# Two products in place of three for four more weight matrices of an encoder layer, and the memory tokens prepared later

## The chip, the core and the metric

The kernel runs on one core of a Trainium2 chip. The metric is the device time of one execution in microseconds (us); lower is better. The kernel before takes 1872.16 us, the median of 3 runs (1871.98 to 1872.21).

## What is computed

One layer of a hybrid encoder on 256 tokens of 2048 features, all in float32, with 256 memory tokens:

```python
for i in range(DEPTH):                       # DEPTH is 1
    u = rmsnorm(h, mix_norm[i])
    h = h + ssd_mixer(u, ...)                # w_in, conv, Mamba-2 scan both ways, norm, w_out
    h = h + mem_cross_attention(rmsnorm(h, xattn_norm[i]), mem_n, wq, wkv, wo)   # 4 heads of 512
    h = h + conv_glu_ffn(rmsnorm(h, ffn_norm[i]), w_up, conv_w, conv_b, w_down)
return rmsnorm(h, final_norm)
```

`mem_n` is the rmsnorm of the memory tokens. `w_out` has 4096 x 2048 weights, `wq` and `wo` 2048 x 2048, `wkv` 2048 x 4096 (keys, then values), `w_up` 2048 x 11264, `w_down` 5632 x 2048.

## The kernel before

**Operands in two parts.** Every float32 operand is split into two float32r parts: a high part (a cast, ScalarE, `split_plain` L106 or `split_scaled` L101) and a low part (operand minus high part, VectorE, L107 or L102). A product of two operands is high x high + high x low + low x high. An activation operand lives in "units": `new_unit` (L94) gives a tile of 4 feature tiles by 2 parts by 256 tokens, high and low side by side; a pool holds 11 of them.

**Weights** stream from HBM in loads of 512 KB (`load_raw` L109, ring of 5 `raw` tiles), are split into `w_hi` and `w_lo` (128 x 1024 each, rings of 4), and go to TensorE as the stationary operand in blocks of 128 x 128. SyncE (SP) issues these loads in order.

**Two forms of the product with features on the partitions.** For each weight block, `gemm_feat` (L132) issues three products with 256 columns: `w_hi` with the operand's high part, `w_hi` with its low part, `w_lo` with the high part (L152 to L154). A `psg` tile of two PSUM banks takes 4 feature tiles, so 512 output features. `gemm_feat_wide` (L157) issues two: `w_hi` with both parts at once, 512 columns (L169), and `w_lo` with the high part, 256 columns (L171). Its output has two halves that must be added (L173 on ScalarE, L174 on VectorE), and a `psg` holds 256 output features. There are two `psg` tiles. Before the change only `w_up` uses the wide form; `w_in`, `w_out`, `wq`, the keys' half of `wkv` and `wo` use three products. Values and `w_down` go through `gemm_tok` (L176), which has the operand stationary and 512 weight columns moving.

**Order of the work.** The source is in program order; a scheduler of the framework then orders each engine's queue by simulated readiness and program priority, and every engine runs its queue in order. Sequence: x is transposed and split; per group of 512 inner features `project` / `project_z` (`w_in`) and `scan_group` (the scan, 8 groups) make one unit `units_y[g]`; `inv_rms` (L223) turns the sum of squares into `r_ssd`, 1/rms of the scan's output, on every partition; the memory tokens are loaded, normed, transposed and split (L491 to L518) in a pool of their own; `w_out` (L527 to L533), whose result is multiplied by `r_ssd`, added to the residual `hT` and split into `units_xa` by `residual_units` (L476); queries, keys, values and attention head by head; `wo`; the FFN. `hT` comes back from DRAM with one 2 MB load (L524).

Of the kernel before, what the change touches and what calls it, by code (L numbers as in the profile page):

```python
# [36 lines left out]
def kernel(  # L37
# [28 lines left out]
    def psum_g():  # L66
        """two banks"""
        return sb(ps_g, [P, 2, 512], "psg")
# [16 lines left out]
    # tri[:, 0, l] = 1 where l >= m, tri[:, 1, l] = 1 where l <= m  # L85
# [46 lines left out]
    def gemm_feat(units, wv, cols, k_first=0, first_raw=None):  # L132
        """features on the partitions: banks of two 128-feature tiles by 256 tokens"""
        width = sum(n for _, n in cols)
        nft = width // P
        kc = 1024 // width
        nk = 4 * len(units)
        ps = psum_g()
        banks = [ps[:, b, :] for b in range((nft + 1) // 2)]
        for k0 in range(0, nk, kc):  # L140
            hi, lo = load_weights(wv, k_first + k0, cols, first_raw if k0 == 0 else None)
            for kk in range(kc):
                kt = k0 + kk
# [12 lines left out]

    def gemm_feat_wide(units, wv, c0, dst):  # L157
        """dst [P, 2, T] = two 128-feature tiles; the high part of the weights meets both parts of the
        operand in one product, so each tile has a bank whose halves add up to it"""
        nk = 4 * len(units)  # L160
        ps = psum_g()
        for k0 in range(0, nk, 4):
            hi, lo = load_weights(wv, k0, [(c0, 2 * P)])
            for kk in range(4):
                kt = k0 + kk
                unit = units[kt // 4]
                for ft in range(2):
                    fs = slice(ft * P, (ft + 1) * P)
                    nc.tensor.matmul(ps[:, ft, :], hi[:, kk, fs], unit[2][:, kt % 4].rearrange("p s t -> p (s t)"),  # L169
                                     start=(kt == 0), stop=False, skip_group_check=True)  # L170
                    nc.tensor.matmul(ps[:, ft, :T], lo[:, kk, fs], unit[0][:, kt % 4, :], start=False,  # L171
                                     stop=(kt == nk - 1), skip_group_check=True)
        nc.scalar.copy(out=dst, in_=ps[:, :, T:])  # L173
        nc.vector.tensor_tensor(out=dst, in0=ps[:, :, :T], in1=dst, op=ALU.add)  # L174

    def gemm_tok(units, wv, c0, k_first=0):  # L176
        """tokens on the partitions: two banks of 128 tokens by 512 features"""
# [23 lines left out]
    def add_square(pool, acc, src2, first):  # L201
        """src2: [P, 2, T]"""
# [7 lines left out]
    def rsqrt_mean(pool, dst, total, n, tags=("rs_v", "rs_s")):  # L210
        """dst = (total / n + eps) ** -0.5: a square root from the table, then one Heron step"""
# [60 lines left out]
        # the column of 1/rms as a row on every partition  # L272
# [12 lines left out]
    with tc.tile_pool(name="ssd", bufs=1) as ssd:  # L285
        acc_y = sb(ssd, [P, 2, T], "acc_y")

# [10 lines left out]
        # log1p(ex) = ln(w) * ex / (w - 1) with w = 1 + ex, and ex itself where w == 1  # L298
# [32 lines left out]
        # decay to the end of the chunk times dt: forward for chunk 0, backward for chunk 1  # L331
# [12 lines left out]
        # exp(cum) where a state comes in: forward rows in chunk 1, backward rows in chunk 0  # L344
# [9 lines left out]
        def conv_silu(banks, f0s, dst):  # L354
            """centred conv of 4 taps over the tokens, bias, silu; two feature tiles per bank"""
# [33 lines left out]
        def scan_group(g, xs, bc, sz):  # L389
# [5 lines left out]
            # token-major x and B  # L395
# [15 lines left out]
            # state that leaves chunk 0 forwards, and the one that leaves chunk 1 backwards  # L411
# [5 lines left out]
            for c in range(2):  # L417
# [8 lines left out]
                # of the two exponents the one of the direction that reaches l from m is <= 0, the other >= 0  # L426
# [14 lines left out]
                # what the incoming state gives, before its decay  # L441
# [34 lines left out]
    def residual_units(pool, hT, banks, u, gname, acc_t, r=None):  # L476
        unit = new_unit()
        for b, bank in enumerate(banks):
            hv = hT[:, u * 4 + 2 * b:u * 4 + 2 * b + 2, :]
            if r is None:  # L480
                nc.vector.tensor_tensor(out=hv, in0=two(bank), in1=hv, op=ALU.add)
            else:
                t = sb(pool, [P, 2, T], "res_t", bufs=2)
                nc.vector.tensor_tensor(out=t, in0=two(bank), in1=rows2(r), op=ALU.mult)
# [5 lines left out]

# [1 line left out]
    units_mem = [new_unit() for _ in range(4)]  # L492
    with tc.tile_pool(name="memp", bufs=1) as memp:
        mt = []
        for tt in range(2):
            m = sb(memp, [P, D], f"mem{tt}")
            nc.sync.dma_start(out=m, in_=mem[tt * P:(tt + 1) * P, :])
            ss = sb(memp, [P, 4], f"mss{tt}")
            for q4 in range(4):
                junk = sb(memp, [P, 512], "junk")  # L500
                nc.scalar.activation(out=junk, in_=m[:, q4 * 512:(q4 + 1) * 512], func=AF.Square,
                                     accum_out=ss[:, q4:q4 + 1])
            rs = sb(memp, [P, 1], f"mrs{tt}")
            tot = sb(memp, [P, 1], f"mtot{tt}")
            nc.vector.tensor_reduce(out=tot, in_=ss, axis=AX.X, op=ALU.add)
            rsqrt_mean(memp, rs, tot, D)
            nc.vector.tensor_scalar(out=m, in0=m, scalar1=rs, scalar2=None, op0=ALU.mult)
            mt.append(m)
        for u in range(4):
            for jj in range(2):  # L510
                ps = psum_m()
                for j in range(2):
                    kt = u * 4 + jj * 2 + j
                    for tt in range(2):
                        nc.tensor.transpose(out=ps[:, j * T + tt * P:j * T + (tt + 1) * P],
                                            in_=mt[tt][:, kt * P:(kt + 1) * P], identity=ident)
                for j in range(2):
                    split_scaled(units_mem[u], jj * 2 + j, two(ps)[:, j, :], pcol("g_mem", u * 4 + jj * 2 + j))  # L518

    with tc.tile_pool(name="res", bufs=1) as res:  # L520
# [4 lines left out]
        with tc.tile_pool(name="att", bufs=1) as att:  # L525
# [4 lines left out]
            for u in range(4):  # L530
                banks = gemm_feat(units_y, w_out_v, [(u * 512, 512)])
                units_xa.append(residual_units(att, hT, banks, u, "g_xa", acc_h, r_ssd))
            inv_rms(att, acc_h, r_xa, D)  # L533

            wkv_v = kview(wkv)
# [4 lines left out]
            # 1/rms of the queries' tokens as columns: it goes into the scale of the softmax  # L540
# [14 lines left out]

            def query(hd):
                return split_banks(pair("q", [P, 4, T]), gemm_feat(units_xa, wq_v, [(hd * 512, 512)]))

            def key(hd):
                return split_banks(pair("k", [P, 4, T]), gemm_feat(units_mem, wkv_v, [(hd * 512, 512)]))  # L560
# [7 lines left out]
            def three(out_ap, lhsT, rhs, first, last):  # L568
                """one product of operands in two parts each; lhsT, rhs: (hi, lo)"""
# [56 lines left out]
            for u in range(4):  # L626
                banks = gemm_feat(units_o, wo_v, [(u * 512, 512)])
                units_ffn.append(residual_units(att, hT, banks, u, "g_ffn", acc_f))
            inv_rms(att, acc_f, r_ffn, D)

# [1 line left out]
        with tc.tile_pool(name="ffn", bufs=1) as ffn:  # L632
# [6 lines left out]
            def ffn_unit(i):  # L639
                sg = sb(ffn, [P, 4, T], "sg")  # L640
                for b in range(2):
                    s = sb(ffn, [P, 2, T], "f_s", bufs=2)
                    gemm_feat_wide(units_ffn, w_up_v, i * 512 + b * 256, s)
# [13 lines left out]
                for b in range(2):  # L657
                    bs = slice(2 * b, 2 * b + 2)
                    s = sb(ffn, [P, 2, T], "f_s", bufs=2)
                    gemm_feat_wide(units_ffn, w_up_v, FFN + i * 512 + b * 256, s)  # L660
# [25 lines left out]
            # the table of the square root, loaded before the last rows need it  # L686
# [70 lines left out]
```

## Time and profile before

| what | value |
|---|---|
| median of 3 runs | 1872.16 us |
| span of the profiled execution (first to last instruction) | 1870.4 us |
| around the span, against the median | 1.8 us |
| TensorE busy | 1851.4 us, 99% |
| VectorE busy | 1246.3 us, 67% |
| ScalarE busy | 1007.2 us, 54% |
| mean granted TensorE clock | 0.998 of 2.4 GHz |

The times in the trace are counted from the first instruction of the span. "Busy" of TensorE is the union of its products' records, which overlap, since a product's record runs on while the next one streams; what a product costs in a stream is therefore read from the distance of starts. The profiled execution has no time of its own beyond its span; the 1.8 us is the difference to the median.

### The profile page before, as it was taken

The page shows a single profiled execution, that of the slowest core. Times are in us where ns is not written, and L with a number is a line of the kernel's source. Part 1 is how long each engine was busy: PE and PEld are TensorE (multiplying, and loading weights), DVE is VectorE, ACT ScalarE, POOL GpSimd, SP SyncE. Part 2 cuts the span into 40 slices and gives each one's busy share as a digit, 9 for nine tenths or more (in the row PEclk, how much of TensorE's full clock was granted, in tenths as well). Part 3 has the DMA queues.
Part 4 walks back from the last instruction along what each step waited for, and adds up shares of the span by engine and source line. Part 5 has one row for each costly group of instructions (what it writes and reads, how often), then busy time and mean ns, then how long its engine had stood idle before and what let it go on. Part 6 is the DMA issues. An engine that isn't in the chain of part 4 may idle for free.

```text
span 1870.4 us, 31851 instructions
## 1 busy us (share of the span) xinstructions
PE 1851.4 (99%) x12845; PEld 1715.6 (92%) x12845; DVE 1246.3 (67%) x1764; ACT 1007.2 (54%) x1434; POOL 2.3 (0%) x11
## 2 busy tenths in 40 slices
PE   8999999999999999999999999999999999999997
PEld 8999999999999999999999998888888888888886
DVE  7778878988887756554454557666664556666654
ACT  6666767766675544444444446555553345555443
POOL 0000000000000000000000000000000000000000
PEclk9999999999999999999999999999999999999999
DMA  8667666766756655555555556566655565656553
GB/s 288 197 201 214 205 197 195 220 199 183 224 183 223 230 188 181 181 161 178 171 178 172 165 182 202 180 189 188 189 191 194 195 192 185 189 184 189 188 195 113
DMA packets 256947, 359.06 MB, mean 192 GB/s; under 512 B 11616, under 2 KB 145120, under 8 KB 256288
## 3 DMA queue, kind: packets, MB, share of 16 engines
q1 hardware_dynamic: 256720, 356.76, 60.8%
q8 instruction: 100, 1.64, 0.4%
q14 instruction: 47, 0.39, 0.1%
q0 software_dynamic: 80, 0.28, 0.0%
HBM read 352.60 MB, written 4.39 MB: 191 GB/s over the span
## 4 chain that ended last, share of the span: by engine, by line
PE 99%; DMA 0%; DVE 0%; ACT 0%; SPq 0%; issue 0%; DVEq 0%
PE psg L169 18%; PE psg L154 17%; PE psg L152 16%; PE psg L153 16%; PE psg L171 9%; PE psm L190 6%; PE psm L191 6%; PE psm L189 6%; PE psm L449 1%; PE psm L444 1%; PE psm L415 1%; PE psm L572 0%; PE psm L570 0%; PE psm L571 0%; DMA x<-in_x_dram 0%; PE psm L401 0%
## 5 line engine op out<-in xcount | busy, mean ns | idle before, releaser
L107 DVE TENSOR_TENSOR w_lo<-raw,w_hi 128x1024 fp32r<-128x1024 f32 x618 | 753.4, 1223 | 518.4 <-ACT w_hi L106 515.7
L106 ACT CAST w_hi<-raw 128x1024 fp32r<-128x1024 f32 x618 | 645.1, 1048 | 697.7 <-PE psg L153 255.0
L154 PE MATMUL psg<-unit,w_lo 128*128 128x256 f32 x2576 | 733.4, 285 | 0.0
L152 PE MATMUL psg<-unit,w_hi 128*128 128x256 f32 x2576 | 731.6, 284 | 0.0
L153 PE MATMUL psg<-unit,w_hi 128*128 128x256 f32 x2576 | 730.3, 284 | 0.0
L154 PEld LDWEIGHTS psg<-unit,w_lo 128*128 128x128 f32 x2576 | 494.3, 192 | 3.4 <-issue 3.1
L152 PEld LDWEIGHTS psg<-unit,w_hi 128*128 128x128 f32 x2576 | 494.4, 192 | 1.7 <-issue 1.7
L153 PEld LDWEIGHTS psg<-unit,w_hi 128*128 128x128 f32 x2576 | 494.5, 192 | 0.3 <-issue 0.2
L169 PE MATMUL psg<-unit,w_hi 128*128 128x512 f32 x1408 | 493.5, 396 | 0.0
L171 PE MATMUL psg<-unit,w_lo 128*128 128x256 f32 x1408 | 393.2, 279 | 0.0
L169 PEld LDWEIGHTS psg<-unit,w_hi 128*128 128x128 f32 x1408 | 264.3, 188 | 63.6
L171 PEld LDWEIGHTS psg<-unit,w_lo 128*128 128x128 f32 x1408 | 265.2, 188 | 0.1
L189 PE MATMUL psm<-w_hi,unit 128*128 128x512 f32 x480 | 186.8, 389 | 0.0
L190 PE MATMUL psm<-w_lo,unit 128*128 128x512 f32 x480 | 186.8, 389 | 0.0
L191 PE MATMUL psm<-w_hi,unit 128*128 128x512 f32 x480 | 186.8, 389 | 0.0
L189 PEld LDWEIGHTS psm<-w_hi,unit 128*128 128x128 f32 x480 | 90.1, 188 | 18.8
L190 PEld LDWEIGHTS psm<-w_lo,unit 128*128 128x128 f32 x480 | 90.1, 188 | 18.6
L191 PEld LDWEIGHTS psm<-w_hi,unit 128*128 128x128 f32 x480 | 90.1, 188 | 18.5
L431 ACT ACTIVATE r<-r,ncum_tok 128x128 f32<-128x128 f32 x128 | 39.4, 390 | 57.7 <-DMA r<-cum_d 55.1
L432 DVE SCALAR_TENSOR_TENSOR r<-r,ncum_tok 128x128 f32<-128x128 f32 x128 | 36.9, 347 | 17.1 <-ACT r L431 17.1
L437 ACT ACTIVATE t<-cb,dt_tok 128x128 f32<-128x128 f32 x128 | 39.1, 388 | 0.7 <-DVE cb L424 0.2
L438 DVE SCALAR_TENSOR_TENSOR t<-cb,dt_tok,t 128x128 f32<-128x128 f32 x128 | 36.5, 348 | 3.3 <-ACT t L437 3.3
(218 smaller groups left out, 1044.7 us busy)
## 6 DMA issues: line engine op xcount, KB each, us to landing
raw<-in_w_up_dram SPq DMA_DIRECT2D x176, 512.0 KB, 3.6
raw<-in_w_in_dram SPq DMA_DIRECT2D x130, 512.0 KB, 4.6
raw<-in_w_down_dram SPq DMA_DIRECT2D x88, 512.0 KB, 3.6
raw<-in_w_out_dram SPq DMA_DIRECT2D x64, 512.0 KB, 4.3
raw<-in_wkv_dram SPq DMA_DIRECT2D x64, 512.0 KB, 3.7
raw<-in_w_in_dram SPq DMA_DIRECT2D x64, 256.0 KB, 4.5
r<-cum_d SPq DMA_DIRECT2D x16, 1024.0 KB, 6.3
raw<-in_wq_dram SPq DMA_DIRECT2D x32, 512.0 KB, 3.6
```

The costliest lines, as they stand in the source:

```text
L106: nc.scalar.copy(out=hi, in_=src)
L107: nc.vector.tensor_tensor(out=lo, in0=src, in1=hi.bitcast(F32), op=ALU.subtract)
L152: nc.tensor.matmul(dst, wh, uh, start=first, stop=False, skip_group_check=True)
L153: nc.tensor.matmul(dst, wh, ul, start=False, stop=False, skip_group_check=True)
L154: nc.tensor.matmul(dst, wl, uh, start=False, stop=last, skip_group_check=True)
L169: nc.tensor.matmul(ps[:, ft, :], hi[:, kk, fs], unit[2][:, kt % 4].rearrange("p s t -> p (s t)"), start=(kt == 0), stop=False, skip_group_ ...
L171: nc.tensor.matmul(ps[:, ft, :T], lo[:, kk, fs], unit[0][:, kt % 4, :], start=False, stop=(kt == nk - 1), skip_group_check=True)
L189: nc.tensor.matmul(banks[tt], uh, hi[:, kk, :], start=(kt == 0), stop=False)
L190: nc.tensor.matmul(banks[tt], uh, lo[:, kk, :], start=False, stop=False)
L191: nc.tensor.matmul(banks[tt], ul, hi[:, kk, :], start=False, stop=(kt == nk - 1))
L431: nc.scalar.activation(out=t1[:, h, :], in_=t1[:, h, :], func=AF.Identity, bias=ncum_tok[:, c, hf:hf + 1])
L437: nc.scalar.activation(out=t2[:, h, :], in_=cb[:, 1, :], func=AF.Copy, scale=dt_tok[:, c, hb:hb + 1])
```

## The change

`w_out`, `wq`, the keys and `wo` go through `gemm_feat_wide`; `w_in` keeps three products. `gemm_feat_wide` now returns its `psg`, and the addition of the halves is a function of its own. `residual_units` calls it for 256 features at a time. The wide form of a weight load is 4 x 256 columns by 128 rows where it was 2 x 512. The preparation of the memory tokens moves from ahead of `w_out` to behind it, and its two 128 x 2048 tiles become four of 128 x 1024 in the buffers of the first head's `k_hi`, `k_lo`, `v_hi`, `v_lo`; the scratch of the squares uses `res_t`. The comments of the source are dropped, so line numbers shift by 3 to 13.

```diff
-    def gemm_feat_wide(units, wv, c0, dst):
+    def gemm_feat_wide(units, wv, cols):
...
-        nc.scalar.copy(out=dst, in_=ps[:, :, T:])
-        nc.vector.tensor_tensor(out=dst, in0=ps[:, :, :T], in1=dst, op=ALU.add)
+        return ps
+
+    def add_halves(dst, ps):
+        nc.scalar.copy(out=dst, in_=ps[:, :, T:])
+        nc.vector.tensor_tensor(out=dst, in0=ps[:, :, :T], in1=dst, op=ALU.add)
...
-    def residual_units(pool, hT, banks, u, gname, acc_t, r=None):
+    def residual_units(pool, hT, units, wv, u, gname, acc_t, r=None):
         unit = new_unit()
-        for b, bank in enumerate(banks):
+        for b in range(2):
+            ps = gemm_feat_wide(units, wv, [(u * 512 + b * 256, 256)])
             hv = hT[:, u * 4 + 2 * b:u * 4 + 2 * b + 2, :]
             if r is None:
-                nc.vector.tensor_tensor(out=hv, in0=two(bank), in1=hv, op=ALU.add)
+                nc.vector.tensor_tensor(out=hv, in0=ps[:, :, T:], in1=hv, op=ALU.add)
+                nc.vector.tensor_tensor(out=hv, in0=ps[:, :, :T], in1=hv, op=ALU.add)
             else:
                 t = sb(pool, [P, 2, T], "res_t", bufs=2)
-                nc.vector.tensor_tensor(out=t, in0=two(bank), in1=rows2(r), op=ALU.mult)
+                add_halves(t, ps)
+                nc.vector.tensor_tensor(out=t, in0=t, in1=rows2(r), op=ALU.mult)
                 nc.vector.tensor_tensor(out=hv, in0=t, in1=hv, op=ALU.add)
...
             for u in range(4):
-                banks = gemm_feat(units_y, w_out_v, [(u * 512, 512)])
-                units_xa.append(residual_units(att, hT, banks, u, "g_xa", acc_h, r_ssd))
+                units_xa.append(residual_units(att, hT, units_y, w_out_v, u, "g_xa", acc_h, r_ssd))
             inv_rms(att, acc_h, r_xa, D)
+            units_mem = [new_unit() for _ in range(4)]
+            mt = []
+            for tt in range(2):
+                halves = [sb(att, [P, 1024], ("k_hi", "k_lo", "v_hi", "v_lo")[2 * tt + hf]) for hf in range(2)]
...
+                for m in halves:
+                    nc.vector.tensor_scalar(out=m, in0=m, scalar1=rs, scalar2=None, op0=ALU.mult)
+                mt.append(halves)
...
+            def split_wide(dst, units, wv, c0):
+                for b in range(2):
+                    t = sb(att, [P, 2, T], "res_t", bufs=2)
+                    add_halves(t, gemm_feat_wide(units, wv, [(c0 + b * 256, 256)]))
+                    split_plain(dst[0][:, 2 * b:2 * b + 2, :], dst[1][:, 2 * b:2 * b + 2, :], t)
+                return dst
+
             def query(hd):
-                return split_banks(pair("q", [P, 4, T]), gemm_feat(units_xa, wq_v, [(hd * 512, 512)]))
+                return split_wide(pair("q", [P, 4, T]), units_xa, wq_v, hd * 512)
...
-                banks = gemm_feat(units_o, wo_v, [(u * 512, 512)])
-                units_ffn.append(residual_units(att, hT, banks, u, "g_ffn", acc_f))
+                units_ffn.append(residual_units(att, hT, units_o, wo_v, u, "g_ffn", acc_f))
```

The change also moves instructions in the queues. Three places follow.

**The end of the scan, VectorE.** `unit_6891` is `units_y[7]`, the last scan unit; `cb_6911` and `r_ssd_89` are the steps of the scan's 1/rms. Before:

```order
L102 SCALAR_TENSOR_TENSOR unit_6891<-xs_5671,par_75,unit_6891 128x256 x4
L107 TENSOR_TENSOR w_lo_7564<-raw_7561,w_hi_7563 128x1024
L208 TENSOR_TENSOR acc_y_303<-acc_y_303,sq_6901 128x512
...
L215 TENSOR_SCALAR cb_6911<-psm_6908 128x256
L217 RECIPROCAL r_ssd_89<-b_tok_6912 128x256
...
L221 RECIPROCAL r_ssd_89<-cb_6911 128x256
L107 TENSOR_TENSOR w_lo_7714<-raw_7711,w_hi_7713 128x1024
```

After, where `psg_6933` and `psg_7120` hold the first two groups of 256 features of `w_out`, and `w_lo_7402` is the fifth weight tile of the third group:

```order
L102 SCALAR_TENSOR_TENSOR unit_6891<-xs_5671,par_75,unit_6891 128x256 x4
L212 TENSOR_TENSOR acc_y_303<-acc_y_303,sq_6901 128x512
L219 TENSOR_SCALAR cb_6911<-psm_6908 128x256
L107 TENSOR_TENSOR w_lo_7358<-raw_7355,w_hi_7357 128x1024
L221 RECIPROCAL r_ssd_89<-b_tok_6912 128x256
L107 TENSOR_TENSOR w_lo_7380<-raw_7377,w_hi_7379 128x1024
...
L225 RECIPROCAL r_ssd_89<-cb_6911 128x256
L178 TENSOR_TENSOR res_t_7110<-psg_6933,res_t_7110 128x512
L178 TENSOR_TENSOR res_t_7297<-psg_7120,res_t_7297 128x512
...
L492 TENSOR_TENSOR hT_6924<-res_t_7110,hT_6924 128x512
...
L107 TENSOR_TENSOR w_lo_7402<-raw_7399,w_hi_7401 128x1024
```

The draining of both `psg` tiles now stands behind the whole 1/rms chain, and the additions to `hT` stand ahead of `w_lo_7402`.

**The loads, SyncE**, around the end of the scan. Before:

```order
L115 DMA raw_7831<-in_w_out_dram 128x2x512
L497 DMA mem0_6928<-in_mem_dram 128x2048
L497 DMA mem1_6952<-in_mem_dram 128x2048
L115 DMA raw_7861<-in_w_out_dram 128x2x512
...
L524 DMA hT_7052<-xT_d_90 128x4096
```

After:

```order
L115 DMA raw_7500<-in_w_out_dram 128x4x256
L502 DMA hT_6924<-xT_d_90 128x4096
L519 DMA k_hi_8462<-in_mem_dram 128x1024
...
L519 DMA v_lo_8490<-in_mem_dram 128x1024
L115 DMA raw_7522<-in_w_out_dram 128x4x256
```

The residual's 2 MB load moves ahead of the memory tokens, and both stand together between two weight loads.

**The memory tokens behind `w_out`, after the change.** On VectorE, from the first half of the tokens' scaling (`k_hi_8462` is the first 128 tokens' first half, `v_hi_8489` the second 128 tokens'; `psg_8596` and `psg_8690` are the query's two groups; `unit_8458` is the first memory unit):

```order
L529 TENSOR_SCALAR k_lo_8463<-k_lo_8463,mrs0_8475 128x1024
L107 TENSOR_TENSOR w_lo_8760<-raw_8757,w_hi_8759 128x1024
L178 TENSOR_TENSOR res_t_8595<-psg_8596,res_t_8595 128x512
...
L225 RECIPROCAL r_xa_6925<-rs_v_8449 128x256
L529 TENSOR_SCALAR v_hi_8489<-v_hi_8489,mrs1_8502 128x1024
L529 TENSOR_SCALAR v_lo_8490<-v_lo_8490,mrs1_8502 128x1024
L107 TENSOR_TENSOR w_lo_8856<-raw_8853,w_hi_8855 128x1024
L178 TENSOR_TENSOR res_t_8689<-psg_8690,res_t_8689 128x512
L102 SCALAR_TENSOR_TENSOR unit_8458<-psm_8516,par_75,unit_8458 128x256
...
L107 TENSOR_TENSOR q_lo_8594<-res_t_8689,q_hi_8593 128x512
L102 SCALAR_TENSOR_TENSOR unit_8458<-psm_8516,par_75,unit_8458 128x256
```

And on TensorE, from the last product of the first query (`psg_8690`) to the second block of the first keys (`psg_8786`):

```order
L171 MATMUL psg_8690<-unit_8067,w_lo_8760 128x256
L537 MATMUL psm_8516<-ident_77,v_hi_8489 128x128
...
L537 MATMUL psm_8543<-ident_77,v_hi_8489 128x128
L169 MATMUL psg_8786<-unit_8458,w_hi_8789 128x512
...
L537 MATMUL psm_8552<-ident_77,k_lo_8463 128x128
L537 MATMUL psm_8552<-ident_77,v_lo_8490 128x128
```

The transposes of the memory tokens, which stood among the products of `w_out`, now stand between the last product of the first query and the first keys, and among the first keys' products.

## Rows read from the trace of the kernel before

**Rows 1.** The page: span, busy time, the chain that ended last.

```profile
span 1870.4 us, 31851 instructions
PE 1851.4 (99%) x12845; PEld 1715.6 (92%) x12845; DVE 1246.3 (67%) x1764; ACT 1007.2 (54%) x1434; POOL 2.3 (0%) x11
PE 99%; DMA 0%; DVE 0%; ACT 0%; SPq 0%; issue 0%; DVEq 0%
```

**Rows 2.** Timeline of TensorE in `w_out`: start us, length, instruction, tiles, form.

```profile
699.73 0.28 PE L154 MATMUL psg<-unit,w_lo 128*128 128x256 f32 x1
...
706.45 0.28 PE L153 MATMUL psg<-unit,w_hi 128*128 128x256 f32 x1
```

**Rows 3.** Stretches of the FFN, L169 alone: length, TensorE busy (count), weight loads.

```profile
1180.00:1380.00 200.00, 200.00 (x578) 108.16 (x578) 1.00 0.61 190
1530.00:1750.00 220.00, 220.00 (x624) 117.06 (x623) 1.00 0.60 187
```

**Rows 4.** Timeline of TensorE, from the end of `wo` into the FFN.

```profile
1122.19 0.28 PE L154 MATMUL psg<-unit,w_lo 128*128 128x256 f32 x1
1122.31 0.40 PE L169 MATMUL psg<-unit,w_hi 128*128 128x512 f32 x1
1122.54 0.28 PE L171 MATMUL psg<-unit,w_lo 128*128 128x256 f32 x1
...
1132.56 0.39 PE L169 MATMUL psg<-unit,w_hi 128*128 128x512 f32 x1
...
1174.62 1.04 PE L671 MATMUL psm<-ident,hT 128*128 128x128 f32 x8
1175.42 0.47 PE L169 MATMUL psg<-unit,w_hi 128*128 128x512 f32 x1
```

**Rows 5.** The chain in order of time, end of the scan: start, length, what.

```profile
574.82 1.24 DVE t L440
576.20 1.09 PE psm L449 x16
589.24 0.43 PE psm L225 x2
```

**Rows 6.** Timeline of VectorE behind it, from the same instruction on.

```profile
575.97 3.49 DVE L107 TENSOR_TENSOR w_lo<-raw,w_hi 128x1024 fp32r<-128x1024 f32 x3
579.37 1.11 DVE L452 SCALAR_TENSOR_TENSOR xs<-xs,par,psm 128x128 f32<-128x128 f32 x4
581.25 1.29 DVE L460 TENSOR_TENSOR xs<-xs,sz 128x512 f32<-128x512 f32 x2
584.20 1.67 DVE L102 SCALAR_TENSOR_TENSOR unit<-xs,par,unit 128x256 fp32r<-128x256 f32 x4
591.08 1.75 DVE L217 RECIPROCAL r_ssd<-b_tok 128x256 f32<-128x256 f32 x1 [0.48 <-ACT b_tok L216]
593.91 0.42 DVE L218 TENSOR_TENSOR cb<-cb,r_ssd 128x256 f32<-128x256 f32 x1
597.11 1.75 DVE L221 RECIPROCAL r_ssd<-cb 128x256 f32<-128x256 f32 x1
```

**Rows 7.** Timeline of SyncE's queue, and the DMA issues (KB each, us to landing).

```profile
598.93 0.82 SPq L497 DMA_DIRECT2D mem<-in_mem_dram  x2
...
hT<-xT_d SPq DMA_DIRECT2D x1, 2048.0 KB, 10.5
```

**Rows 8.** Groups of instructions around the memory tokens: count, busy us, mean ns.

```profile
L507 DVE TENSOR_SCALAR mem<-mem,mrs 128x2048 f32<-128x2048 f32 x2 | 2.6, 1286 | 0.1
L102 DVE SCALAR_TENSOR_TENSOR unit<-psm,par,unit 128x256 fp32r<-128x256 f32 x16 | 6.8, 476 | 0.0
L174 DVE TENSOR_TENSOR f_s<-psg,f_s 128x512 f32<-128x512 f32 x6 | 4.1, 683 | 0.0
L505 DVE TENSOR_REDUCE mtot<-mss 128x1 f32<-128x4 f32 x2 | 0.3, 154 | 0.2 <-ACT junk L501 0.2
```

**Rows 9.** Stretches at the span's end: busy of PE, PEld, DVE, ACT, POOL; granted clock.

```profile
1858.00:1860.00 2.00, 1.23 (x6) 0.69 (x4) 1.33 (x3) 0.72 (x2) 0.00 (x0) 1.00 0.00 0
1860.00:1862.00 2.00, 0.00 (x0) 0.00 (x0) 1.33 (x13) 1.13 (x5) 0.00 (x0) 0.83 0.00 0
1862.00:1864.00 2.00, 0.00 (x0) 0.00 (x0) 1.93 (x6) 0.88 (x2) 0.00 (x0) 0.50 0.37 138
```

**Rows 10.** The chain in order of time, the first transposes of x.

```profile
12.46 0.85 PE psm L256 x4
16.38 0.44 PE psm L256 x4
```

More of the change, by code (lines that the diff above doesn't have):

```diff
@@ L162, in gemm_feat_wide @@
         for k0 in range(0, nk, 4):
-            hi, lo = load_weights(wv, k0, [(c0, 2 * P)])
+            hi, lo = load_weights(wv, k0, cols)
             for kk in range(4):
@@ L489, in residual_units @@
         return unit
[L492 to L518, printed above, removed]
     with tc.tile_pool(name="res", bufs=1) as res:
@@ L530 @@
             for u in range(4):
-                banks = gemm_feat(units_y, w_out_v, [(u * 512, 512)])
-                units_xa.append(residual_units(att, hT, banks, u, "g_xa", acc_h, r_ssd))
+                units_xa.append(residual_units(att, hT, units_y, w_out_v, u, "g_xa", acc_h, r_ssd))
             inv_rms(att, acc_h, r_xa, D)
+            units_mem = [new_unit() for _ in range(4)]
+            mt = []
+            for tt in range(2):
+                halves = [sb(att, [P, 1024], ("k_hi", "k_lo", "v_hi", "v_lo")[2 * tt + hf]) for hf in range(2)]
+                mss = sb(att, [P, 4], f"mss{tt}")
+                for hf, m in enumerate(halves):
+                    nc.sync.dma_start(out=m, in_=mem[tt * P:(tt + 1) * P, hf * 1024:(hf + 1) * 1024])
+                    for q4 in range(2):
+                        junk = sb(att, [P, 512], "res_t", bufs=2)
+                        nc.scalar.activation(out=junk, in_=m[:, q4 * 512:(q4 + 1) * 512], func=AF.Square,
+                                             accum_out=mss[:, 2 * hf + q4:2 * hf + q4 + 1])
+                rs = sb(att, [P, 1], f"mrs{tt}")
+                tot = sb(att, [P, 1], f"mtot{tt}")
+                nc.vector.tensor_reduce(out=tot, in_=mss, axis=AX.X, op=ALU.add)
+                rsqrt_mean(att, rs, tot, D, (f"mv{tt}", f"ms{tt}"))
+                for m in halves:
+                    nc.vector.tensor_scalar(out=m, in0=m, scalar1=rs, scalar2=None, op0=ALU.mult)
+                mt.append(halves)
+            for u in range(4):
+                for jj in range(2):
+                    ps = psum_m()
+                    for j in range(2):
+                        kt = u * 4 + jj * 2 + j
+                        for tt in range(2):
+                            nc.tensor.transpose(out=ps[:, j * T + tt * P:j * T + (tt + 1) * P],
+                                                in_=mt[tt][kt // 8][:, (kt % 8) * P:(kt % 8 + 1) * P], identity=ident)
+                    for j in range(2):
+                        split_scaled(units_mem[u], jj * 2 + j, two(ps)[:, j, :], pcol("g_mem", u * 4 + jj * 2 + j))
             wkv_v = kview(wkv)
@@ L554, in split_banks @@
                 return dst
+            def split_wide(dst, units, wv, c0):
[4 more added lines that the diff above has]
+                return dst
             def query(hd):
-                return split_banks(pair("q", [P, 4, T]), gemm_feat(units_xa, wq_v, [(hd * 512, 512)]))
+                return split_wide(pair("q", [P, 4, T]), units_xa, wq_v, hd * 512)
             def key(hd):
-                return split_banks(pair("k", [P, 4, T]), gemm_feat(units_mem, wkv_v, [(hd * 512, 512)]))
+                return split_wide(pair("k", [P, 4, T]), units_mem, wkv_v, hd * 512)
             def value(hd):
@@ L642, in ffn_unit @@
                     s = sb(ffn, [P, 2, T], "f_s", bufs=2)
-                    gemm_feat_wide(units_ffn, w_up_v, i * 512 + b * 256, s)
+                    add_halves(s, gemm_feat_wide(units_ffn, w_up_v, [(i * 512 + b * 256, 256)]))
                     nc.vector.tensor_tensor(out=s, in0=s, in1=rows2(r_ffn), op=ALU.mult)
@@ L659, in ffn_unit @@
                     s = sb(ffn, [P, 2, T], "f_s", bufs=2)
-                    gemm_feat_wide(units_ffn, w_up_v, FFN + i * 512 + b * 256, s)
+                    add_halves(s, gemm_feat_wide(units_ffn, w_up_v, [(FFN + i * 512 + b * 256, 256)]))
                     nc.vector.tensor_tensor(out=s, in0=s, in1=rows2(r_ffn), op=ALU.mult)
```

## The prediction

> **What bounds the kernel now.** I read the page first. TensorE is busy for 1851.4 of 1870.4 us, and the chain that ended last is TensorE for 99% [rows 1]. So a change is worth what it takes out of TensorE's stream, less the idle time that it opens there. The predicted time is the span plus the 1.8 us between the span and the median of the runs.
>
> Next come the prices of the stream, read from the distance of starts, since records overlap. In `w_out` there are 56 products of the three-product form after the first row shown, up to the last: 6.72 / 56 = 0.120 us each, 0.360 per weight block [rows 2]. A wide pair has two rhythms. In the FFN's first half 578 pairs take 200 us, so 0.3467 each (200 / 577); in its second half 624 take 220 us, 0.3531 [rows 3]. The timeline shows where each begins: entered straight from a three-product stream, 29 distances take 10.25 us, 0.3534; the quicker rhythm begins behind eight transposes [rows 4]. A converted block therefore gains 6.7 ns (slow) to 13.4 ns (fast).
>
> Then I looked for idle time. Around the change there is one, before the product at 576.20, which waits for VectorE's step at 574.82 [rows 5]. It is the scan, and it stays. What matters behind it is VectorE's queue, which works nearly without a gap from 574.82 until the 1/rms of the scan is done at 598.86 [rows 5, 6]. TensorE did not feel this before.
>
> **What the products gain.** `w_out` has 32 x 16 = 512 blocks, `wq`, keys and `wo` 256 each: 1280. The first 128 blocks of `w_out` end with the scan's last unit, which comes no sooner, so 1152 count. Of these I take 640 as slow, since they are entered from score and attention products or from `w_out`'s own slow stream (640 x 6.7 = 4.3 us), and 512 at 10 ns, the middle of both, since transposes or an idle TensorE stand ahead of them (5.1). Sum 9.4; bounds 1152 x 6.7 = 7.7 and 1152 x 13.4 = 15.4.
>
> **A: the third group of `w_out` waits for a `psg`.** A `psg` used to hold 512 features and now holds 256, and there are still two. Before, the first `psg` took all products up to the scan's end and the second stood free. Now both are full when the last unit has been multiplied, and the third must wait until VectorE has added the halves of one. In the new order these additions stand behind the whole 1/rms chain. TensorE's side: the sums of squares begin at 589.24 and take 0.86 [rows 5]; of the 384 products of the first 512 features 14 follow in the order, 1.7 us, so TensorE is done at 591.7. The wide form comes to the same, because it waits for the last unit. VectorE's side, from 590.1: 0.4 of hand-over, a `w_lo` at 1.16 (a third of 3.49), a reciprocal 1.75, a `w_lo` 1.16, three small steps 1.1, a reciprocal 1.75 [rows 6], the addition 0.68 by L174 [rows 8]: 598.1. Idle **6.4 us**. If both `w_lo` find room earlier, 4.1; if the chain ends as late as before, 598.9, with one `w_lo` more and the addition behind it, 9.0.
>
> **The residual's load.** `hT` (2 MB, 10.5 us from issue to landing [rows 7]) now stands in SyncE's queue behind a wait for the same reciprocal at which the memory tokens were issued at 598.93, but its first user, L492, stands ahead of a `w_lo` of the third group in VectorE's queue. From 597.5 it lands at 608.0. The third group's first four weight tiles are 32 pairs at 0.35 and last until 598.1 + 11.2 = 609.3; behind the landing stand two additions (L492) at 0.68 and the `w_lo` at 1.16, done at 610.5, and with 0.2 of hand-over TensorE waits **1.4 us**. Bounds 0 (the load is issued sooner) and 4 (the weight loads beside it slow it). SyncE's queue then has four token loads ahead of the next weights; a ring of five covers them, and they cost nothing unless the ring has run empty, which the 4 takes in.
>
> **B: the memory tokens.** Their 32 transposes stood among the products of `w_out` and cost only their own time, which they keep. Now they must be normed between `w_out`'s end and the first keys, and TensorE has only the first query to cover this: 64 pairs at 0.35, the sums of the 1/rms 0.86, four transposes 0.44 [rows 5, 10], 23.7 us. VectorE has, in that stretch of the new order up to the scaling of the second 128 tokens: seven `w_lo`, 8.1; six passes over 512 columns at 0.68, 4.1; a 1/rms with two reciprocals, 5.0; 14 small steps at 0.154, 2.2; four scalings at half of 1286 ns, 2.6; two low parts at 0.476, 1.0 [rows 6, 8]. That is 23.0, and it waits for TensorE and ScalarE several times in the norms; the one such wait with rows, 592.83 to 593.91, is 1.08 [rows 6], and I take 3.8 in all: 26.8. TensorE is idle for 3.1. Twelve transposes then end at 28.1, while the first memory unit needs another scaling, a `w_lo`, an addition and a low part (0.64 + 1.16 + 0.68 + 0.48): 29.7, 1.6 more. The next transposes want a bank whose low part stands behind the query's: 1.1. Sum **5.8 us**, bounds 0 (VectorE is in time) and 9 (none of the 3.8 beside other work, twice).
>
> **The clock.** At the end of the span TensorE's granted clock reads 1.00, then 0.83, then 0.50 (2.4 and 1.2 GHz) in the three stretches after its last products [rows 9], and at the beginning four transposes took 0.85 us, 3.9 us later 0.44 [rows 10]. The waits of A and B are long idle times of that kind. A return costs at most half of 3.9 us, 2.0; I take 1.2 for each, 2.4 (bounds 0 and 4). The Trainium skill, "TensorE: Matmul & The Clock Gate", section "Why this matters for your kernels", says that idle gaps between bursts of products bring the lower clock back; rows 9 agree, and no row before has a gap inside the kernel that is long enough to show it.
>
> **Nothing** for the rest: ScalarE does the same casts and one more copy per `psg` (busy 54%), the attention's and `wo`'s groups have 5 us and more of products between two uses of a `psg` against 3 of draining, and `w_in` with the scan is unmoved. The FFN's two halves may change rhythm, since their transposes stand elsewhere: 614 pairs x 6.7 ns is 4.1 either way, taken as 0.
>
> **Sum.** 6.4 + 1.4 + 5.8 + 2.4 = 16.0 lost, 9.4 gained, so the span goes from 1870.4 to 1877.0, and the time to **1878.8 us**.
>
> **The rivals.** *VectorE is in time* (other side): it decides whether the second 128 tokens are scaled before TensorE ends the query, at 23.7 us after `w_out`; then B is 0, and if the same slack lets both `w_lo` of A go ahead and `hT` arrive in time, only 4.1 is lost and the clock stays: 1872.2 + 4.1 - 9.4 = 1866.9. For it speaks that VectorE is busy for only 67% [rows 1]; against it, the sum of 23.0 busy us in 23.7. *Tokens in time, but A as summed*: 6.4 + 1.4 + 1.2 - 9.4, so 1871.8. *The fast rhythm everywhere*, the FFN's second half included: gain 15.4 + 4.1, so 1868.7; for it, that the FFN's first half holds it for 200 us [rows 3]; against it, that the streams here are entered from three products [rows 4]. *The slow rhythm everywhere*, the FFN's first half too: gain 7.7, 4.1 lost there, 1884.6. *Only the columns count*: both forms stream 768 per block, so nothing is gained and the stalls remain, 1888.2; rows 2 to 4 speak against it. The Trainium skill, the same page, section "Back-to-back issue gap", gives each product its columns and a fixed 2.5 ns; by it the saved product is worth 2.5 ns and all 1280 blocks 3.2 us (an estimate). The rows' 6.7 to 13.4 ns differ from that.
>
> **How the numbers follow.** A measurement of this kernel can tell about 0.2%, 3.7 us, from no change: faster is below 1868.4, slower above 1875.9. My forecast has 0.47; of it 0.38 lie above 1875.9, and 0.09, with A and B near their lower ends, within the band. VectorE in time 0.13 (faster); tokens in time with A 0.10 (same); fast everywhere 0.10, half faster, half same; slow everywhere 0.17 and columns alone 0.03 (slower). So faster 0.18, same 0.24, slower 0.58. The range is 1866.5 to 1886.0: it takes in all but the columns and the outer ends of A, B and the clock. The likeliest case's own range is 1873 to 1885.
>
> **What would show it.** Right: L169 and L171 in `w_out`, `wq`, keys and `wo` at 0.347 to 0.353 per pair; TensorE idle for some 6 us near 592 to 598, ended by VectorE's addition L178; VectorE waiting at L492 for the load of `hT`; TensorE idle before the transposes L537 and before the first keys, ended by VectorE's L529 and L102; the granted clock below 1.00 behind both. Wrong: pairs at 0.360; L178 ahead of the reciprocals in time; a scaling that ends before the query's last product; idle time at `wo` or in the FFN that was not there.

## The result, and the profile after

The changed kernel takes 1883.84 us, the median of 4 runs (1882.20 to 1885.48); the kernel before beside it 1872.07 (1870.69 to 1872.21). The ratio is 1.0064, with a 95% interval of 1.0050 to 1.0078: **slower by 11.8 us**, where 6.7 was forecast.

The page of the profile after: the span, and the line of busy time that answers to [rows 1].

```profile
span 1882.1 us, 29344 instructions
...
PE 1845.0 (98%) x11565; PEld 1653.2 (88%) x11565; DVE 1267.7 (67%) x1798; ACT 1019.9 (54%) x1458; POOL 2.3 (0%) x11
```

TensorE issues 1280 products fewer, is busy for 6.4 us less, and the span is 11.7 longer: the change did what it says, and TensorE now stands idle. Its timeline shows where; the bracket at a row's end is the idle time ahead of it and what ended it. The end of the scan and of the first 512 features of `w_out`:

```profile
571.80 0.39 PE L171 MATMUL psg<-unit,w_lo 128*128 128x256 f32 x1 [1.20 <-DVE w_lo L107]
576.35 0.39 PE L171 MATMUL psg<-unit,w_lo 128*128 128x256 f32 x1 [1.50 <-DVE w_lo L107]
589.53 0.59 PE L169 MATMUL psg<-unit,w_hi 128*128 128x512 f32 x1 [3.46 <-DVE unit L102]
606.92 0.77 PE L169 MATMUL psg<-unit,w_hi 128*128 128x512 f32 x1 [9.12 <-DVE res_t L178]
```

And between the first query and the first keys:

```profile
769.86 0.33 PE L537 MATMUL psm<-ident,v_hi 128*128 128x128 f32 x1 [1.74 <-DVE v_hi L529]
772.65 0.51 PE L169 MATMUL psg<-unit,w_hi 128*128 128x512 f32 x1 [1.26 <-DVE unit L102]
774.52 0.45 PE L537 MATMUL psm<-ident,k_lo 128*128 128x128 f32 x1 [0.90 <-DVE unit L102]
```

Together 19.2 us; before there was 1.37 at the product of 576.20 [rows 5]. The large one, 9.12, ends with VectorE's addition of the halves, L178.

Stretches of L169 after, with the granted clock as the third number from the right:

```profile
590.00:592.00 2.00, 1.97 (x4) 1.07 (x4) 0.50 0.67 234
592.00:594.00 2.00, 1.98 (x6) 1.06 (x5) 0.70 0.00 0
594.00:596.00 2.00, 1.37 (x6) 0.64 (x5) 1.00 0.00 0
606.00:608.00 2.00, 1.06 (x2) 0.62 (x2) 0.50 0.95 242
608.00:610.00 2.00, 1.96 (x4) 0.99 (x3) 0.50 0.99 418
610.00:612.00 2.00, 1.99 (x6) 1.13 (x6) 0.93 0.92 393
774.00:776.00 2.00, 0.74 (x1) 0.50 (x2) 0.53 0.27 106
776.00:778.00 2.00, 1.79 (x4) 0.82 (x3) 0.62 0.00 0
```

Behind the waits of 3.46 and 9.12, and behind the three at the tokens, the clock is at its lower level, and 4 pairs fit into 2 us where 6 do at 1.00. Busy time times what the clock lacks gives the loss. TensorE works nearly throughout these stretches (2 us each; 1.1 of the one at 606, 1.5 of the one at 774): 1.0 + 0.6, 0.55 + 1.0 + 0.15, and 0.7 + 0.75, so some **4.8 us** in all.

The chain of waits after, end of the scan (start, length, what):

```profile
559.72 0.27 DVE t L444
560.00 7.98 DMA r<-cum_d
...
570.61 1.14 DVE w_lo L107
...
575.16 1.15 DVE w_lo L107
...
582.26 1.02 PE psm L453 x16
...
595.42 0.43 PE psm L229 x2
...
597.62 1.28 ACT L220
...
601.04 1.16 DVE w_lo L107
...
603.35 1.76 DVE r_ssd L225
...
605.47 0.59 ACT res_t L177
606.09 0.70 DVE res_t L178
```

The scan's last product (L453) starts at 582.26, where it was 576.20, and the sums of squares at 595.42, where they were 589.24 [rows 5]: 6.2 us later. From the end of the sums, 596.3, the chain takes 10.5 us to the end of L178 at 606.8, and the third group starts at 606.92, 15.2 us behind the 591.7 at which the kernel before went on.

The gain is in the distance of starts. L169 in `w_out` and in the FFN's two halves:

```profile
620.00:740.00 120.00, 120.00 (x341) 63.88 (x340) 1.00 0.58 190
1200.00:1380.00 180.00, 180.00 (x520) 97.17 (x520) 1.00 0.60 190
1540.00:1740.00 200.00, 200.00 (x567) 106.40 (x566) 1.00 0.59 186
```

`w_out` runs at 120 / 340 = 0.3529 per pair (slow), the FFN's halves at 0.3468 and 0.3534, as before [rows 3].

**The account.** Idle 19.2 - 1.4 = 17.8, the clock 4.8, together 22.6 lost. Of the 1152 blocks behind the first group about half went in each rhythm: `w_out`, three heads' keys and, by the starts of its L169, 41 blocks of the first query slow (384 + 192 + 41 = 617), the rest of the queries, the first keys and `wo` quick (535). 617 x 6.7 ns is 4.1 us and 535 x 13.3 is 7.1, so 11.2 gained. Net 11.4; the spans differ by 11.7.

### The profile page after: what moved, and what is told of

The parts are those of the page before. It is cut to its first block, busy times and chain, and to the rows that moved or that the text cites. A ratio compares the mean times of both kernels' runs of the same rounds, so it can differ in the third digit from the quotient of the medians.

```text
span 1882.1 us, 29344 instructions
## 1 busy us (share of the span) xinstructions
PE 1845.0 (98%) x11565; PEld 1653.2 (88%) x11565; DVE 1267.7 (67%) x1798; ACT 1019.9 (54%) x1458; POOL 2.3 (0%) x11
## 4 chain that ended last, share of the span: by engine, by line
PE 97%; DVE 1%; DMA 1%; ACT 0%; issue 0%; SPq 0%; DVEq 0%; ACTq 0%
PE psg L169 33%; PE psg L171 17%; PE psg L154 8%; PE psg L153 8%; PE psg L152 8%; PE psm L194 6%; PE psm L195 6%; PE psm L193 6%; PE psm L453 1%; PE psm L419 1%; PE psm L448 1%; DMA r<-cum_d 0%; PE psm L586 0%; PE psm L585 0%; PE psm L584 0%; DMA x<-in_x_dram 0%
## 5 line engine op out<-in xcount | busy, mean ns | idle before, releaser
L169 PE MATMUL psg<-unit,w_hi 128*128 128x512 f32 x2688 | 947.7, 397 | 13.8 <-DVE res_t L178 9.1
L169 PEld LDWEIGHTS psg<-unit,w_hi 128*128 128x128 f32 x2688 | 506.2, 188 | 131.2 <-issue 9.7
L152 PE MATMUL psg<-unit,w_hi 128*128 128x256 f32 x1296 | 369.4, 285 | 0.0
L153 PE MATMUL psg<-unit,w_hi 128*128 128x256 f32 x1296 | 368.3, 284 | 0.0
L152 PEld LDWEIGHTS psg<-unit,w_hi 128*128 128x128 f32 x1296 | 249.5, 193 | 1.7 <-issue 1.7
L153 PEld LDWEIGHTS psg<-unit,w_hi 128*128 128x128 f32 x1296 | 249.5, 193 | 0.0
```

## The experiments

Each time is a median, with the ratio to the kernel before on the same chip and its 95% interval. T1 is my theory, that the wait for a `psg` at the end of the scan is the main loss.

### First group of `w_out` in three products (e1)

```diff
...
             for u in range(4):
-                units_xa.append(residual_units(att, hT, units_y, w_out_v, u, "g_xa", acc_h, r_ssd))
+                banks = gemm_feat(units_y, w_out_v, [(u * 512, 512)]) if u < 1 else None
+                units_xa.append(residual_units(att, hT, units_y, w_out_v, u, "g_xa", acc_h, r_ssd, banks))
```

> Only the first 512 features of w_out go back to three products in one psg tile of 512 features; all else is as in the changed kernel. Theory T1 (two psg tiles of 256 features are both full until the 1/rms of the scan is done, and their draining stands behind it in VectorE's queue): the waits of TensorE at 570.2, 574.5, 585.8 and 597.5 us (1.2 + 1.5 + 3.5 + 9.1, less 1.4 that the kernel before has too) and the half clock behind them (some 3.5) go, 17.4 us, while the waits for the memory tokens stay: 1866 us. Rival T2 (the cost comes from moving the memory tokens and the residual's load together): the wait stays, about 1883 us. Rival T3 (the weight tiles of 4 x 256 come late, whatever takes the results): the wait comes back at the third group, about 1880 us.

Measured 1867.95 us, ratio 0.9977 (0.9968 to 0.9987). The stretch of all engines in which the changed kernel had its two long waits:

```profile
588.00:608.00 20.00, 20.00 (x133) 18.31 (x132) 15.46 (x18) 9.18 (x10) 0.00 (x0) 1.00 0.66 215
```

TensorE is busy for all of the 20 us at full clock. Leaving the first 128 blocks in the old form gives back 15.9 us, of the 17.4 that T1 gave, and more than the 11.8 of the whole loss: T1 holds, and what the wide form gains elsewhere shows. T2 and T3 fall for the larger part of the loss.

### Third group in two small PSUM tiles (e2)

```diff
-    def gemm_feat_wide(units, wv, cols):
+    def gemm_feat_wide(units, wv, cols, small=False):
         nk = 4 * len(units)
-        ps = psum_g()
+        ps = [psum_m(), psum_m()] if small else psum_g()
...
-            ps = gemm_feat_wide(units, wv, [(u * 512 + b * 256, 256)])
+            ps = gemm_feat_wide(units, wv, [(u * 512 + b * 256, 256)], r is not None and (u, b) == (1, 0))
```

> As the changed kernel, but the third group of 256 features of w_out collects in two of the small psum tiles (psm) and so needs no psg. T1: the 9.1 us before the third group and the half clock behind it (1.7) go, the earlier waits stay: 1873 us, and TensorE starts the third group's products near 598 us, as soon as the sums of squares have been multiplied. T2: no change in time, 1883 us. T3: TensorE starts the third group at 598 but waits within it for w_lo, about 1880 us.

Measured 1871.42 us, ratio 0.9996 (0.9987 to 1.0005). The timeline of TensorE: the last wait of the scan, the last pair of the second group, the first of the third.

```profile
590.20 0.79 PE L167 MATMUL psg<-unit,w_hi 128*128 128x512 f32 x1 [3.46 <-DVE unit L102]
...
599.37 0.28 PE L169 MATMUL psg<-unit,w_lo 128*128 128x256 f32 x1
599.49 0.39 PE L167 MATMUL psm<-unit,w_hi 128*128 128x512 f32 x1
```

The third group follows without a gap, although VectorE's queue is as late as ever. So the 9.12 us were the wait for the tile, nothing else. The earlier waits stay, as T1 said. The median is 1.6 below T1's 1873, inside the spread of the runs (1869.09 to 1873.25). In the profiled execution, which took 1872.73, `w_out` ran in the quick rhythm (319 pairs from 630 to 740 us, where the changed kernel has 313). The expectation did not reckon with that; whether the other executions had it is not known.

### Memory tokens ahead of `w_out` (e3), and both edits (e4)

The block that prepares the tokens is moved, unchanged, from behind the loop over `u` to ahead of it; e4 adds the edit of e1.

```diff
+            units_mem = [new_unit() for _ in range(4)]
+            mt = []
...
             w_out_v = kview(w_out)
...
             inv_rms(att, acc_h, r_xa, D)
-            units_mem = [new_unit() for _ in range(4)]
-            mt = []
...
```

> As the changed kernel, but the memory tokens are prepared ahead of w_out in program order, still in the room of k and v. T1: only the waits for the tokens go (1.7 + 1.3 + 0.9 idle, some 2 at half clock), the wait at the end of the scan stays: 1878 us. T2: nearly all of the loss goes, 1866 us or less.

> Both edits of the runs before: first 512 features of w_out in three products, memory tokens ahead of w_out. T1: the parts add up, 1883.8 - 17.4 - 6 = 1860 us, which is the kernel before less 1152 blocks at 6.7 to 13.4 ns (7.7 to 15.4 us). T2: as e3 alone. If the two waits hide one another, the time is above 1863.

e3 took 1893.57 us, ratio 1.0113 (1.0098 to 1.0128): 15 us above what T1 expected, and the wrong way for T2. The timeline of TensorE behind the sums of squares:

```profile
598.55 0.28 PE L171 MATMUL psg<-unit,w_lo 128*128 128x256 f32 x1
621.38 1.09 PE L529 MATMUL psm<-ident,k_hi 128*128 128x128 f32 x4 [22.55 <-ACT res_t L177]
```

I had not looked at where the transposes come to stand. With the wide first group they follow at once on the end of the first 512 features, ahead of the third group, and wait there for their load (issued behind the scan's 1/rms, 8.6 us to landing for the first piece) and for the norm. They add 13 us to the wait that they were to leave alone. As I read the order, what brings them forward is the same lack of a free `psg`: nothing else is ready there.

e4 took 1863.73 us, ratio 0.9956 (0.9941 to 0.9971). With the first group in three products the transposes stand 165 products behind that group's end, and the two edits together gain 20.1 us, where e1 alone gained 15.9 and e3 alone lost 9.7. Against the 1860 expected it has one new wait, for a cast on ScalarE that stands behind the squares of the tokens:

```profile
616.50 0.47 PE L169 MATMUL psg<-unit,w_hi 128*128 128x512 f32 x1 [2.10 <-ACT w_hi L106]
```

### `w_out` alone in two products (e5)

From the kernel before: only `w_out` goes through `gemm_feat_wide`; `wq`, keys, `wo` and the tokens stay.

```diff
...
-                banks = gemm_feat(units_y, w_out_v, [(u * 512, 512)])
-                units_xa.append(residual_units(att, hT, banks, u, "g_xa", acc_h, r_ssd))
+                units_xa.append(residual_units(att, hT, None, u, "g_xa", acc_h, r_ssd, units_y, w_out_v))
```

> One part of the change alone: the kernel before with only w_out in two products; wq, keys, wo in three, memory tokens ahead of w_out in their own room. The 32 transposes of the tokens stand 9 products behind the scan's last sums of squares in TensorE's order, ahead of the third group of w_out. T1 (both psg full) together with T4 (from e3: the transposes wait there for the tokens' loads and norm): the wait at the end of the scan becomes longer than the changed kernel's 9.1 us, some 20 us, and 384 blocks give back 2.6 to 5.1: 1888 to 1894 us. T2 (the move of the tokens is what costs): w_out alone gains 512 blocks and nothing waits, 1866 to 1869 us.

Measured 1904.24 us, ratio 1.0169 (1.0154 to 1.0185): the direction of T1 and T4, and 10 more than their 1894. TensorE's timeline has five waits in a row, 22.6 us:

```profile
616.77 1.09 PE L516 MATMUL psm<-ident,mem 128*128 128x128 f32 x4 [18.83 <-ACT junk L502]
619.40 2.82 PE L516 MATMUL psm<-ident,mem 128*128 128x128 f32 x12 [1.54 <-DVE mem L508]
622.51 2.19 PE L516 MATMUL psm<-ident,mem 128*128 128x128 f32 x12 [0.29 <-DVE unit L102]
625.17 0.63 PE L516 MATMUL psm<-ident,mem 128*128 128x128 f32 x4 [0.46 <-DVE unit L102]
627.25 0.80 PE L169 MATMUL psg<-unit,w_hi 128*128 128x512 f32 x1 [1.46 <-DVE res_t L174]
```

All 32 transposes stand ahead of the third group, at half clock (12 in 2.82 us, where they take 1.31 in e4), and the earlier waits of 1.7, 1.5 and 3.5 us are here too; the expectation reckoned with one wait of 20. So the move of the tokens behind `w_out` is not the loss of this change: beside a wide first group it saves 9.7 us (e3 against the changed kernel).

### `w_out` in three products, the rest wide (e6)

The edit of e1 for all four `u`, with the tokens ahead of `w_out`; the lines are against e4.

```diff
-                banks = gemm_feat(units_y, w_out_v, [(u * 512, 512)]) if u < 1 else None
+                banks = gemm_feat(units_y, w_out_v, [(u * 512, 512)]) if u < 4 else None
```

> All of w_out in three products, wq, keys and wo in two, memory tokens prepared ahead of w_out in the room of k and v. No wait is expected at the end of the scan or before the keys, so this shows the gain by itself: 576 blocks in the fast rhythm (13.3 ns) and 192 in the slow (6.7), 9.0 us: 1863 us. If a wide product gives back only what its saved gap is on the Trainium skill's page TensorE: Matmul & The Clock Gate (2.5 ns, 768 blocks, 1.9 us): 1870 us.

Measured 1864.56 us, ratio 0.9960 (0.9945 to 0.9975): 7.1 us gained (4.7 to 10.3). That holds the 9.0 worked out from the rhythms and excludes the 1.9 worked out from 2.5 ns per product. The Trainium skill, "TensorE: Matmul & The Clock Gate", section "Back-to-back issue gap", gives those 2.5 ns for the isolated gap and says itself that a stream of weight loads and products keeps another spacing; here the measurement decides.

### The wait filled (e7)

```diff
+            if r is not None and (u, b) == (1, 0):
+                fill = psum_m()
+                for _ in range(80):
+                    nc.tensor.transpose(out=fill[:, :P], in_=units[7][1][:, 3, :P].bitcast(F32), identity=ident)
             ps = gemm_feat_wide(units, wv, [(u * 512 + b * 256, 256)])
```

> As the changed kernel, but 80 transposes of 128 x 128, whose result nobody reads, stand ahead of the third group of w_out, where TensorE waits for 9.1 us; at 0.109 us each they take 8.7. Theory C (the half clock behind the wait, 0.64 us per pair, comes of the wait): the pairs behind it run at 0.35 at once, 1.7 us less: 1882 us, and the granted clock stays at 1.00 there. Rival: the clock is lowered by something else, and the time stays at 1884 or grows by what the transposes overrun.

Measured 1882.89 us, ratio 1.0062 (1.0047 to 1.0077); against the changed kernel's 1883.84 that is within the spread. The rows show the clock to be what theory C says. TensorE's timeline, and the stretches behind the filled wait:

```profile
599.25 8.90 PE L486 MATMUL psm<-ident,unit 128*128 128x128 f32 x80
608.54 0.47 PE L169 MATMUL psg<-unit,w_hi 128*128 128x512 f32 x1 [0.39 <-DVE res_t L178]
```

```profile
608.00:610.00 2.00, 1.61 (x10) 1.32 (x9) 2.00 (x4) 0.16 (x1) 0.00 (x0) 1.00 0.83 287
610.00:612.00 2.00, 2.00 (x14) 1.75 (x13) 0.19 (x1) 0.53 (x1) 0.00 (x0) 1.00 1.01 434
```

The granted clock is 1.00 where it was 0.50. The times cannot show the saving: the medians differ by 1.0 us, and the four runs lie between 1881.15 and 1886.14. The profiled execution is the slowest of them. In it the rhythms moved too: `w_out` ran quick (347 pairs from 620 to 740 us, where the changed kernel has 341), and the FFN's first half, which the edit does not touch, slow. Its L169:

```profile
1200.00:1380.00 180.00, 180.00 (x511) 95.73 (x510) 1.00 0.61 186
```

That is 0.3529 per pair, where the changed kernel had 0.3468. The stream has 629 pairs, which take 221.9 us from first to last start, where the changed kernel's took 217.7: 4.2 us lost in this execution. What the other three did is not known.

### The rhythm (e8, e11)

On e4. e11 has one transpose in place of four.

```diff
+            turn = psum_m()
+            for _ in range(4):
+                nc.tensor.transpose(out=turn[:, :P], in_=h_tok[:, 1, 1536:1664], identity=ident)
             units_h = [ffn_unit(i) for i in range(6, 11)]
```

> As e4 (first group of w_out in three products, tokens ahead of w_out), with four transposes whose result nobody reads 25 products behind the beginning of the FFN's second half. Theory R (the rhythm of a wide stream is set at its entry, and a burst of transposes sets it anew): the second half goes from 0.3533 to 0.3467 us per pair, 620 x 6.7 ns = 4.1 us less 0.4 for the transposes: 1860 us where e4 had 1863.7. Rival (the slow rhythm belongs to that half, its loads or its tiles): unchanged but for 0.4, 1864 us.

> As e8 with one transpose in place of four at the same place. If any other product between the pairs sets the rhythm anew, the second half runs at 0.3467 from there and the time is 0.3 below e8's 1860.7; if it takes a burst, the second half stays at 0.3533 and the time is e4's, 1863.8.

e8 took 1860.69 us, ratio 0.9942 (0.9925 to 0.9958); e11 1862.72, ratio 0.9949 (0.9935 to 0.9963). L169 in the FFN's second half, in e4, e8 and e11:

```profile
1530.00:1730.00 200.00, 200.00 (x567) 106.36 (x566) 1.00 0.61 186
```

```profile
1530.00:1730.00 200.00, 200.00 (x578) 107.87 (x578) 1.00 0.62 190
```

```profile
1530.00:1730.00 200.00, 200.00 (x568) 106.37 (x567) 1.00 0.60 186
```

Four transposes that do nothing turn 0.3534 (200 / 566) into 0.3466 (200 / 577); one does not. Each kernel has one trace, so the rhythm could be chance; but this half ran slow in all ten traces without the four transposes (both kernels, e1 to e7, e11), and quick in all three with them (e8, e9, e10). So Theory R holds for a burst of four at this place; in between nothing was tried. The times alone do not show it: the intervals of e4, e8 and e11 overlap. Between e8 and e11 the medians differ by 2.0 us; the rows of the second half, 627 pairs at 6.6 ns, ask for 4.2 less the transposes.

### The tokens later in `w_out` (e9, e10)

On e8, the block of the tokens goes behind the first (e9) or second (e10) group of `w_out`.

```diff
                 units_xa.append(residual_units(att, hT, units_y, w_out_v, u, "g_xa", acc_h, r_ssd, banks))
+                if u == 0:
+                    units_mem = [new_unit() for _ in range(4)]
...
```

> As e8 (first group in three products, four transposes in the FFN's second half), with the preparation of the memory tokens behind the first group of w_out in program order rather than ahead of it. In e4 and e8 TensorE waited 2.1 to 2.3 us at 614 to 619, for casts of weights on ScalarE behind the squares of the tokens, whose load was late. If the later place moves the squares behind those casts, 1858.5 us; if the squares stand where they stood, 1860.7.

> As e9, with the tokens behind the second group of w_out: the loads have 20 us more. Theory: the 2.2 us wait goes, 1858.5 us, and the transposes still end before the keys. Rival: the last transposes wait for units that are free only late in w_out, or the tokens' scaling is late again at the keys, 1860 us or more.

e9 took 1857.56 us, ratio 0.9921 (0.9907 to 0.9935); e10 1857.32, ratio 0.9918 (0.9905 to 0.9932). From the scan's end into the FFN, in e9, all engines:

```profile
577.00:1380.00 803.00, 803.00 (x4631) 705.74 (x4627) 515.14 (x617) 406.33 (x524) 0.00 (x0) 1.00 0.61 189
```

TensorE has no idle time left in 803 us; the wait of 2.1 to 2.3 us is gone in both, as expected. These two beat both kernels: 15 us below the one before, 26 below the changed one.

## Why the prediction was right, and where its sizes were off

The sign, the places and the range (1866.5 to 1886.0) held; the size did not: 6.7 forecast, 11.8 measured. That the time still fell inside the range is in part luck. The losses came to 22.6 where 16.0 were forecast: A and the clock were larger by 9.9, of which 4.8 are waits that no term of the sum names, while B and the residual's load were smaller by 3.3 and the gain larger by 1.8.

- **Gain, 9.4 forecast, 11.2 by the rows.** The prices per block are those of [rows 3]. The share of the quick rhythm was larger: the queries, taken as slow because they are entered from score products, ran quick but for 41 blocks of the first, and so did `wo`.
- **A, 6.4 forecast, 9.1 + 4.8** (1.20 + 1.50 + 3.46, less the 1.37 of before). The mechanism is the one forecast, shown by e2: L178 behind the 1/rms, `psg` not free. The step that failed is that "the wide form comes to the same, because it waits for the last unit", by which the first 512 features end at 591.7. They ended at 597.8, since the scan itself became late. The chain shows two waits for a `w_lo` (1.20, 1.50) that stands in VectorE's queue between the steps of the scan, behind the load of `r` that landed at 568.0, and the scan's last product 6.1 us late. In TensorE's order 41 pairs now stand ahead of it, 41 x 0.35 = 14.4 us, where 104 products at 0.120 stood, 12.5; and this stretch began 2.3 us later already (564.46, before 562.12). Then TensorE ran dry for 3.46 us ahead of the last unit. Every kernel with a wide first group that was run has the 3.46 (e2, e3, e5 and e7 as the changed one); e1, e4 and e6, with three products there, do not. Which of the two, the `w_lo` or the order, came first was read from the rows and not tried alone.
- **The 1/rms and the addition, 8.0 us forecast (590.1 to 598.1), 10.5 measured.** ScalarE's table load for the root (1.28, L220) stood in the chain, behind a cast, and its copy of the second half (0.59, L177) ahead of the addition; the sum had neither. In the kernel before the same table load ran at 589.03, before the sums of squares had ended, and so cost the chain nothing.
- **The residual's load, 1.4 forecast, 0.** VectorE did wait for it, as said:

```profile
613.23 1.29 DVE L492 TENSOR_TENSOR hT<-res_t,hT 128x512 f32<-128x512 f32 x2 [4.65 <-DMA hT<-xT_d]
```

  but the third group began 8.8 us later than forecast, so its fifth weight tile was not yet wanted. One wait hid the other.
- **B, 5.8 forecast, 3.9.** The three waits are the three of the sum: 3.1, 1.6 and 1.1 forecast, 1.74, 1.26 and 0.90 measured, ended by L529 and L102 as said. The 3.8 us that the sum gave VectorE for waiting rests on a misread stretch: from 592.83 to 593.91 VectorE did not wait, it made a `w_lo`, in a row that [rows 6] leaves out. In the changed kernel it waited for 2.8 in all up to the second scaling. The row of the kernel before:

```profile
592.77 1.23 DVE L107 TENSOR_TENSOR w_lo<-raw,w_hi 128x1024 fp32r<-128x1024 f32 x1
```

- **The clock, 2.4 forecast, 4.8.** A return costs 1.5 to 1.7, not 1.2, and there were three, since the wait for the last unit was not forecast. The Trainium skill, "TensorE: Matmul & The Clock Gate", section "Why this matters for your kernels", says that idle gaps between bursts of products bring the lower clock back: the runs agree, with 0.50 behind 9.12 us of waiting and 1.00 when e7 filled it.
- **The rivals.** Columns alone falls: e6 gains 7.1 us. Slow or quick everywhere falls: both rhythms stand side by side in one run. VectorE in time falls by the waits. The FFN's halves did not change rhythm, as taken, but e7 shows that they can without an edit there.

## What to carry to other kernels

When a product's result takes twice the PSUM per feature, count how long the tiles that are left hold TensorE while their drain stands behind something else, and keep the old form just there: 128 of 1280 blocks cost more than all the others gained. An engine at 67% busy can still be what TensorE waits for at a stage's end, and a stall ahead of a queue's wait makes the later places of the sum shift too, so work them out one from another. Before an edit that moves a block in program order, look where its instructions come to stand on each engine (e3).

## What the runs showed of the hardware

The rhythm of a wide stream, 0.3467 or 0.3533 us per pair, holds for hundreds of pairs and can be set by what comes between: four transposes set the slow one quick (e8, and again in e9 and e10), one did not (e11). What else sets it stays open: in e7, whose edit lies 570 us ahead of the FFN, a stream of 629 pairs in the first half came out slow, where all other traces have it quick. It is worth some 4 us in such a stream, more than the edits themselves may move. The granted clock was at half behind idle times of 3.46 and 9.12 us, and behind three of 1.74, 1.26 and 0.90 with short bursts between them; behind one of 2.10 us (e4) it stayed at 1.00:

```profile
614.00:616.00 2.00, 0.40 (x3) 0.09 (x1) 1.54 (x7) 2.00 (x8) 0.00 (x0) 1.00 1.10 348
616.00:618.00 2.00, 1.50 (x9) 1.34 (x10) 2.00 (x6) 2.00 (x4) 0.00 (x0) 1.00 1.10 349
```

The length of a wait alone does not tell. Behind a wait of 1.48 or 1.49 us at the scan's last product the clock fell to 0.50 in e1 and e8, and stayed at 1.00 in e4, e6, e10 and e11; each had a shorter wait some 2 us ahead of it, 0.76 and 0.36 in the first two, 0.15 to 0.60 in the others. What decides it stays open. In e1:

```profile
580.00:582.00 2.00, 2.00 (x13) 1.67 (x10) 2.00 (x2) 0.34 (x1) 0.00 (x0) 0.50 0.48 130
```
